# A written-out order for all four compute engines in the RWKV-7 stage of an encoder trunk

## The chip, the cores and the metric

One core of a Trainium2 chip runs the whole program in one launch. The metric is device time in microseconds from start to end of an execution; the median of three runs stands for the kernel.

## What is computed

Two layers on a sequence of 256 tokens of width 1024. Layer 0 mixes tokens by a bidirectional RWKV-7 recurrence, layer 1 by dilated attention; each is followed by a mixture of 32 experts of which a token uses two. Every sub-layer is normalised, shifted, scaled and gated by vectors that are products of c with large matrices (the modulations). The change touches layer 0's recurrence alone:

```python
xx = 0.5 * (x_prev + x_next) - h
xs = h[:, :, None, :] + xx[:, :, None, :] * mu          # six mixes: r, k, v, w, a, g
r, k, v = xs[..., 0..2] @ w_rkv
decay, a, g = low-rank functions of xs[..., 3..5], one for each direction
def step(state, inp):                                   # 16 heads of 64, forward and backward
    sa = einsum('bhvk,bhk->bhv', state, a_t)
    state = state * w_t + sa * b_t + v_t * k_t
    y_t = einsum('bhvk,bhk->bhv', state, r_t)
o = sum over directions of g * (groupnorm(y) + bonus);  out = o @ w_o
```

## The kernel before

**Stages.** Input loads and the first modulations; normalisation and the mixes; the recurrence (`rwkv`); the experts of layer 0, whose 96 weight blocks of 1 MB stream in; attention; the experts of layer 1.

**The recurrence.** 16 heads go as 8 head pairs (index i), both directions (z) at once, in four chunks of 64 tokens. For a pair: the products k, r and v (`keys`, `values`) as three fp16 matmuls each in place of one fp32, from weights and mixes that ACT and DVE or POOL have split into a high and a low half (`split`, `w16`, `halves`, L441 to L449); `rates` (decay and in-context rate); `scale_keys` (two scans L857, BK L880, AR L887 and L888); `chunks` (the matrices G, evicted by DVE as GV and GI, L920; Ah on ACT and Al on POOL, L931 and L932; BT, R2, UV; `bonus`, sT); `inverse` (a triangular inverse by doubling in PSUM banks "iv": PE, then ACT's T and X at L992, then DVE's Q at L1014, six levels); `recur` (four steps R, U, S, Y in banks "ch"); `finish` (group norm by a root of nine small DVE instructions, L345 to L354; yn L1162; oT L1163). Buffers such as AR, GI, BT and UV exist twice (pools `odd` and `even`), so pair i waits for pair i-2.

**What sets the order.** Each of these is a Python generator. `weave` runs them as streams with one clock of its own, `now`, to which it adds an estimate of PE's work; a stream yields the time it thinks it must wait; among ripe streams the one of lowest `RANK` goes next. Within the stage PE's instructions keep the order in which they are made (`on_pe`, `tc.keep_in_program_order`). DVE, ACT and POOL are ordered by the compiling scheduler, by `tc.cur_priority`, which `weave` sets from `now` and `OFFSET`.

**The modulations.** `modulation_flow` takes 48 tiles of 512 KB (`aring`, two slots) and for each adds `w * silu` to `acc` on DVE in two halves of 512 columns (`ada_add`, L374 for the first of eight, L376 for the others), one tile each `PACE` = 4.0 of `weave`'s clock. The loads of `aring` and of the weights (`wring`) are issued by SP in order. When the last pair's products and the modulations are done, `releases` frees pools, in which expert weights are then loaded ahead; more is freed as the last pairs pass.

**The run-up.** Before `weave`: mixes k and r on DVE, the first pair's k and r in fp32, `hidden` with mix w on DVE (pAR) and mix a on ACT and POOL (pUV, L646 and L647), and rates(0). In `weave`, `supply` first does mix v and its split, the splits of k and r, and `hidden_gate` (mix g on ACT and POOL, then 32 hg matmuls).

## Time and profile before

| | us |
|---|---|
| median of three runs (lowest, highest) | 1209.1 (1204.81, 1210.89) |
| the profiled execution: its time | 1205.22 |
| the profiled execution: its span | 1203.4 |
| run-up of the recurrence | 58 to 106 |
| its steady part | 106 to 450 |

Engines: PE = TensorE matmul, PEld = its weight loads, DVE = VectorE, ACT = ScalarE, POOL = GpSimd, SP = SyncE. In the rows below, the page's first part gives busy us, share and instructions; a stretch gives its bounds and length, busy us of each engine with its instructions, PE's mean granted clock, the DMA engines' busy share and GB/s; a group of instructions gives line, engine, operation, tiles, shapes and count, then busy us and mean ns, then the idle time before them and what ended it; a wait gives who waited for whom, us in total, times and the longest; a tile's or line's instructions give their shortest, median and longest duration in ns and their first and last start in us; the timeline gives start, duration, instruction and count, merged where equal ones follow each other, with the idle time before in brackets. A PE that is busy here isn't at its peak, since ends of matmuls are modelled.

### The profile page before, as it was taken

Reading aid. Unit: us, or ns where it says so; the run is one execution under the profiler, and the core shown is the slowest. Engines: PE = TensorE matmul, PEld = TensorE weight load, DVE = VectorE, ACT = ScalarE, POOL = GpSimd, SP = SyncE. Lnnn points to the kernel's source line nnn. Section 1 sums busy time; section 2 is a strip of 40 time slices with the busy share of each in tenths; the row PEclk is TensorE's granted clock in tenths of the full one; section 3 lists DMA queues with packets and bytes.
Section 4 is the critical chain, followed back from the end, with each engine's and each line's share of the span. In section 5 each row is a group of like instructions: output and inputs, shape, how many; then the busy total and the mean of one; then the engine's idle time right before and its main releaser. Section 6 shows DMA issues by size and latency. Waiting matters only on the chain.

```text
span 1203.4 us, 25449 instructions
## 1 busy us (share of the span) xinstructions
PE 1008.3 (84%) x10740; PEld 678.5 (56%) x10740; DVE 674.5 (56%) x1446; ACT 469.0 (39%) x955; POOL 219.7 (18%) x142
## 2 busy tenths in 40 slices
PE   4639778898787989878988989899879999789886
PEld 4527566776565654533433368677768754344432
DVE  6895886687877644412221177988985663122112
ACT  3555565665555442100010176555454631010002
POOL 4472122311312320000000023112292100000000
PEclk9969898988889998998999989998999999899989
DMA  9444344134414287898999996878653599989995
GB/s 368 145 157 146 128 129 137 63 112 145 146 54 142 111 337 282 351 419 352 421 422 420 419 419 233 308 268 327 228 174 130 213 357 373 417 367 421 421 422 223
DMA packets 53199, 322.05 MB, mean 268 GB/s; under 512 B 5922, under 2 KB 6562, under 8 KB 21458
## 3 DMA queue, kind: packets, MB, share of 16 engines
q1 hardware_dynamic: 51986, 315.88, 67.4%
q0 software_dynamic: 800, 3.36, 0.7%
q8 instruction: 89, 1.46, 0.5%
q10 hardware_dynamic: 288, 1.05, 0.3%
q14 instruction: 36, 0.29, 0.1%
HBM read 319.22 MB, written 1.05 MB: 266 GB/s over the span
## 4 chain that ended last, share of the span: by engine, by line
PE 50%; DVE 26%; DMA 12%; ACT 6%; issue 4%; SPq 0%; POOL 0%; ACTq 0%; DVEq 0%; POOLq 0%
PE gu L271 9%; PE qkv L271 8%; DMA wring<-in_w_moe_dram 7%; DVE acc L376 5%; DMA aring<-in_w_ada_dram 5%; PE dn L271 4%; PE xT L271 4%; PE acc L271 4%; PE wo L271 4%; PE iv L271 3%; DVE wl L449 2%; PE kr L271 2%; PE ada L271 2%; PE warm L271 1%; DVE BK L880 1%
## 5 line engine op out<-in xcount | busy, mean ns | idle before, releaser
L271 PE MATMUL gu<-wring,xT 128*32 128x512 f32 x1024 | 134.1, 624 | 15.6 <-DMA wring<-in_w_moe_dram 11.0
L376 DVE SCALAR_TENSOR_TENSOR acc<-aring,silu,acc 128x512 f32<-128x512 f32 x140 | 125.4, 932 | 15.6 <-DMA aring<-in_w_ada_dram 15.3
L443 POOL TENSOR_TENSOR wl<-wring,wh 128x1024 f16<-128x1024 f32 x24 | 57.0, 2379 | 413.0 <-DMA wring<-in_w_qkv_dram 247.1
L271 PE MATMUL qkv<-hh,wl 128*128 128x256 f16 x384 | 106.3, 277 | 2.0 <-DVE wl L449 2.0
L271 PE MATMUL qkv<-hh,wh 128*128 128x256 f16 x384 | 106.4, 277 | 1.8 <-ACT hh L1758 1.8
L271 PE MATMUL qkv<-hl,wh 128*128 128x256 f16 x384 | 106.0, 277 | 1.8 <-DVE hl L1759 1.8
L271 PEld LDWEIGHTS gu<-wring,xT 128*32 128x32 f32 x1024 | 31.2, 113 | 100.3 <-issue 91.1
L449 DVE SCALAR_TENSOR_TENSOR wl<-wring,wh 128x1024 f16<-128x1024 f32 x56 | 74.3, 1330 | 16.9 <-ACT wh L445 16.8
L271 PEld LDWEIGHTS <-wh 128*128 128x128 f16 x768 | 76.4, 100 | 12.9 <-issue 3.5
L271 PE MATMUL dn<-wring,hidT 128*32 128x256 f32 x1024 | 64.5, 398 | 18.5 <-ACT hidT L1561 18.4
L271 PE MATMUL acc<-y,back 128*128 128x512 f32 (+1 forms) x144 | 67.8, 595 | 10.3 <-DVE y L1588 8.1
L1363 DVE SCALAR_TENSOR_TENSOR sg<-sg,gu 128x256 f32<-128x256 f32 x16 | 6.7, 420 | 121.5 <-ACT sg L1362 121.5
L445 ACT ACTIVATE wh<-wring 128x1024 f16<-128x1024 f32 x56 | 58.6, 1050 | 35.8 <-PE qkv L271 28.3
L271 PEld LDWEIGHTS xT<-oh,x 128*128 128x128 f32 x512 | 59.0, 192 | 21.1 <-PE gu L271 9.2
L1588 DVE TENSOR_TENSOR y<-dn,ga 128x512 f32<-128x512 f32 x28 | 19.4, 692 | 89.3 <-PE dn L271 60.1
L1362 ACT ACTIVATE sg<-gu 128x256 f32<-128x256 f32 x16 | 6.1, 384 | 152.7 <-PE gu L271 152.7
L271 PE MATMUL xT<-oh,x 128*128 128x128 f32 x512 | 63.5, 280 | 2.5 <-DVE oh L1472 2.5
L271 PEld LDWEIGHTS dn<-wring,hidT 128*32 128x32 f32 x1024 | 31.4, 113 | 48.4 <-ACT hidT L1561 22.2
L1504 ACT ACTIVATE back<-bT 128x256 f32<-128x256 f32 x16 | 6.2, 386 | 132.0 <-PE acc L271 132.0
L271 PEld LDWEIGHTS <-w 128*128 128x128 f16 x528 | 50.9, 102 | 10.3 <-issue 0.5
L271 PE MATMUL qkv<-wl,hh 128*128 128x256 f16 x192 | 53.3, 278 | 1.3 <-POOL wl L443 1.3
L271 PE MATMUL qkv<-wh,hl 128*128 128x256 f16 x192 | 53.4, 278 | 0.0
(356 smaller groups left out, 2214.8 us busy)
## 6 DMA issues: line engine op xcount, KB each, us to landing
wring<-in_w_moe_dram SPq DMA_DIRECT2D x192, 1024.0 KB, 19.8
aring<-in_w_ada_dram SPq DMA_DIRECT2D x96, 512.0 KB, 4.1
wring<-in_w_qkv_dram SPq DMA_DIRECT2D x36, 1024.0 KB, 9.2
wring<-in_w_kr_dram SPq DMA_DIRECT2D x8, 1024.0 KB, 5.8
wring<-in_w_vl_dram SPq DMA_DIRECT2D x8, 640.0 KB, 4.5
wring<-in_w_rwo_dram SPq DMA_DIRECT2D x4, 1024.0 KB, 6.2
wring<-in_w_ato_dram SPq DMA_DIRECT2D x4, 1024.0 KB, 6.9
x<-in_x_dram POOLq DMA_DIRECT2D x2, 512.0 KB, 7.7
```

The lines of the kernel that those rows point to most:

```text
L271: return on_pe(nc.tensor.matmul(out=o, lhsT=lhsT, rhs=rhs, start=start, stop=stop, **kw))
L376: V.scalar_tensor_tensor(out=acc[:, s], in0=w[:, s], scalar=silu[:, k:k + 1], in1=acc[:, s], op0=ALU.mult, op1=ALU.add)
L443: eng.tensor_tensor(out=lo, in0=src, in1=hi, op=ALU.subtract)
L445: A.activation(out=hi, in_=src, func=AF.Copy, scale=by)
L449: V.scalar_tensor_tensor(out=lo, in0=src, scalar=by, in1=hi, op0=ALU.mult, op1=ALU.subtract)
L880: V.tensor_tensor(out=BK[:, :, par::2, o:o + 64], in0=src.rearrange("p z (c t) -> p z c t", c=4)[:, :, par::2], in1=e2[:, :, par::2], op=A ...
L1362: A.activation(out=o, in_=ps[:, 0:256], func=AF.Tanh, scale=0.5)
L1363: V.scalar_tensor_tensor(out=o, in0=o, scalar=1.0, in1=ps[:, 0:256], op0=ALU.add, op1=ALU.mult)
L1504: A.activation(out=back, in_=ps[:, 0:S], func=AF.Copy)
L1588: V.tensor_tensor(out=y, in0=py[c], in1=gates[i, 5][:, c * 512:(c + 1) * 512], op=ALU.mult)
```

## The change

It replaces `RANK`, `OFFSET` and `weave`'s one clock by an account: for each engine the time at which it is free, for each tile when it was written and by whom, for each PSUM bank when it was last read. DVE, ACT and POOL are wrapped, so that inside `weave` each of their instructions, too, keeps the order in which it is made. A stream yields the engine and the tiles or banks that its next step needs; `weave` runs the step that can start first by the account. An instruction of DVE, ACT or POOL costs a fixed part and a part for each column (`COST`, in microseconds), a hand-over to another engine `HAND`. The account holds no loads.

Besides, work is moved. Mix w goes from DVE to ACT and POOL. Of each modulation tile DVE keeps one half, and POOL does the other with two instructions (one for the first of eight), no earlier than 4n + 2 on the account's clock. The splits become a stream of their own (`conversions`), the gate's mix and matmuls another that begins when the splits of xk and of kr's second half are done; pair 0's v is an fp32 product. Pairs 1 and later wait for the gate before GI. `inverse` begins after Ah (`matrices`) and not after all of `chunks`; sT comes last. Y leaves `recur` for a stream with a bank "yy"; "ch" has one bank left. The load of g1 comes after kr 1.

```diff
-RANK = dict(X=0, C=1, R=2, F=3, D=4, G=5, S=6, H=6, W=7, A=2.5)
-OFFSET = dict(X=0, C=-6, R=-4, F=-2, D=-2, G=-1, S=0, H=0, W=0, A=8)
+GIVE_WAY = dict(X=0, C=0, R=0, D=0.1, Y=0.2, F=0.3, G=0, K=0, S=0.1, B=0.3, H=0, W=0.5, A=0.3)
+COST = dict(V=(0.16, 0.00105), A=(0.19, 0.0008), P=(0.15, 0.00217))
+HAND = dict(T=0.3, V=0.15, A=0.15, P=0.15)
+SWITCH = 0.1
...
+    def account(e, t, outs, ins):
+        start = free[e]
+        for n in ins:
+            w = wrote.get(n)
+            if w:
+                start = max(start, w[0] + (0.0 if w[1] == e else HAND[w[1]]))
+        for n in outs:
+            w = wrote.get(n)
+            if w and w[1] != e:
+                start = max(start, w[0] + HAND[w[1]])
+        free[e] = end = start + t
...
+            def call(*args, **kw):
+                i = f(*args, **kw)
+                if pinned[0]:
+                    tc.keep_in_program_order(i)
...
+                        a, b = COST[self.e]
+                        n = max(int(np.prod(v.shape[1:])) for v in outs)
+                        account(self.e, a + b * n, [v.tensor.name for v in outs], [v.tensor.name for v in ins])
...
         while live:
+            best = None
             for s in live:
...
+                t = start_of(s)
+                if t is None:
+                    continue
+                v = t + GIVE_WAY[s[1]] - (SWITCH if s is last and s[3][0] == "T" else 0.0)
+                if best is None or v < best[0]:
+                    best = (v, t, s)
...
-        ctx2.enter_context(banks(pp=2, ps=2, iv=2, ch=2))
+        ctx2.enter_context(banks(pp=2, ps=2, iv=2, ch=1, yy=1))
...
-                if j in (4, 5):
+                if j in (3, 4, 5):
+                    yield ("A",)
                     A.activation(out=out[k], in_=xx[:, k], func=AF.Copy, scale=mu)
                     P.tensor_tensor(out=out[k], in0=out[k], in1=h[:, k], op=ALU.add)
...
         def hidden_gate():
-            xg, _ = passing(5, "BT")
+            nonlocal oT
+            yield after(("half", 1), ("conv", 1))
+            _, xg = place_of((odd, "GI"), (odd, "BT"))
+            yield from mix_steps(5, xg)
...
+        def first_values():
+            yield after(("room", 2))
+            xv = [v[:, k * S:(k + 1) * S] for v in f32v for k in range(4)]
+            yield from mix_steps(2, xv)
...
+            for k in range(KD):
+                mm(ps[:, 0:S], wv[:, k], xv[k], start=(k == 0), stop=(k == KD - 1))
...
+            yield after(("hidden_gate", 0 if i else -1))
             GI = turns(i, [128, 2, 2, 4, 64], "GI")
...
-            yield after(("ready", i))
-            yield 1.0
+            yield after(("matrices", i))
+            yield ("V", A16[2 * (i % 2)])
...
-            for i, m, k in ADA_RWKV:
+            for n, (i, m, k) in enumerate(ADA_RWKV):
                 w = modulations.take((i, m, k))
...
-                ada_add(acc, w, k, k == 0)
-                yield PACE
+                for e, by in ((1, V), (0, P)):
+                    yield (by.e, PACE * n + 2.0)
+                    a, v = acc[e], w[:, e * 512:e * 512 + 512]
+                    if k == 0:
+                        by.tensor_scalar(out=a, in0=v, scalar1=silu[:, k:k + 1], scalar2=None, op0=ALU.mult)
+                    elif e:
+                        V.scalar_tensor_tensor(out=a, in0=v, scalar=silu[:, k:k + 1], in1=a, op0=ALU.mult, op1=ALU.add)
+                    else:
+                        P.tensor_scalar(out=v, in0=v, scalar1=silu[:, k:k + 1], scalar2=None, op0=ALU.mult)
+                        P.tensor_tensor(out=a, in0=v, in1=a, op=ALU.add)
...
-        streams = dict(X=releases(), C=recurrences(), R=inverses(), F=finishes(), D=readies(), G=last_gates(),
-                       S=supply(), W=outputs(), A=modulation_flow())
+        streams = dict(X=releases(), C=recurrences(), R=inverses(), D=readies(), Y=results(), F=finishes(),
+                       G=last_gates(), K=conversions(), S=supply(), B=hidden_gate(), W=outputs(), A=modulation_flow())
```

## Rows read from the trace of the kernel before

**Rows 1.** The page: span, and busy us (share) of each engine.

```profile
span 1203.4 us, 25449 instructions
PE 1008.3 (84%) x10740; PEld 678.5 (56%) x10740; DVE 674.5 (56%) x1446; ACT 469.0 (39%) x955; POOL 219.7 (18%) x142
```

**Rows 2.** Busy time by stretch: run-up, steady part, expert stage.

```profile
58.00:106.00 48.00, 26.47 (x175) 21.61 (x175) 45.00 (x62) 21.47 (x38) 30.14 (x19) 0.75 0.47 165
...
106.00:450.00 344.00, 290.02 (x5078) 223.12 (x5077) 245.35 (x563) 198.11 (x411) 82.69 (x56) 0.91 0.38 133
...
500.00:520.00 20.00, 18.52 (x172) 9.21 (x168) 5.11 (x14) 2.55 (x7) 0.00 (x0) 1.00 1.01 422
```

**Rows 3.** The chain of waits from 106 to 450 us, shares by line.

```profile
by line: DVE acc L376 9.4%; PE iv L271 9.0%; DMA aring<-in_w_ada_dram 7.1%; PE kr L271 6.0%; issue 5.0%; PE wo L271 3.5%; DVE BK L880 3.4%; PE ada L271 3.2%; DVE Q L1014 3.0%; PE R L271 2.7%; PE S L271 2.5%; PE G L271 2.3%; PE v L271 2.0%; 
```

**Rows 4.** Groups of DVE instructions from 106 to 450 us.

```profile
L376 DVE SCALAR_TENSOR_TENSOR acc<-aring,silu,acc 128x512 f32<-128x512 f32 x70 | 60.5, 892 | 9.2 <-DMA aring<-in_w_ada_dram 8.9
...
L374 DVE TENSOR_SCALAR acc<-aring,silu 128x512 f32<-128x512 f32 x10 | 6.0, 626 | 0.0
```

**Rows 5.** Who waited for whom, from 58 to 476 us.

```profile
PE iv L271 <- DVE Q L1014: 14.8, 9, 4.0
...
DVE acc L376 <- DMA aring<-in_w_ada_dram: 10.9, 10, 2.0
...
PE R L271 <- DVE SD L1092: 8.4, 8, 2.6
```

**Rows 6.** Shortest, median and longest duration of four DVE instructions, their starts.

```profile
L376 DVE SCALAR_TENSOR_TENSOR acc<-aring,silu,acc x70: 736/747/2600, 137.9 to 396.3; 128x512 f32<-128x512 f32 x70
...
L1003 DVE TENSOR_TENSOR X<-Ah,cst x8: 412/426/2353, 103.4 to 415.6; 128x512 f16<-128x512 f16 x8
...
L880 DVE TENSOR_TENSOR BK<-kd,e x16: 416/420/1483, 83.2 to 387.8; 128x256 f32<-128x256 f32 x16
...
L920 DVE TENSOR_TENSOR GV<-G,cstr x32: 409/416/429, 92.2 to 409.7; 128x256 f32<-128x256 f32 x32
```

**Rows 7.** The timeline of the run-up, 46 to 94 us.

```profile
46.37 10.66 POOL L647 TENSOR_TENSOR pUV<-pUV,hT 128x256 f32<-128x256 f32 x8 [9.50 <-ACT pUV L646]
...
52.28 7.30 DVE L649 SCALAR_TENSOR_TENSOR pAR<-xx,colr,hT 128x256 f32<-128x256 f32 x7
...
71.89 1.23 PE L271 MATMUL L<-hidw,wring 64*128 64x256 f32 x4 [7.78 <-DVE kss L793]
...
87.92 5.77 PE L271 MATMUL hg<-pBT,wring 128*128 128x256 f32 x16
```

**Rows 8.** A group of POOL instructions from 58 to 476 us.

```profile
L566 POOL TENSOR_TENSOR wring<-wring,ga 128x512 f32<-128x512 f32 x16 | 21.7, 1390 | 34.8 <-DMA wring<-in_w_rwo_dram 34.8
```

**Rows 9.** The POOL group without an input, whole span.

```profile
L721 POOL MEMSET eb<- 128x528 f32 x1 | 0.5, 537 | 8.1 <-DVE pUV L376 8.1
```

**Rows 10.** The timeline of DVE and of POOL near 346 us.

```profile
345.76 1.48 DVE L880 TENSOR_TENSOR BK<-kd,e 128x256 f32<-128x256 f32 x1
347.17 1.48 DVE L880 TENSOR_TENSOR BK<-bb,e 128x256 f32<-128x256 f32 x1
...
343.95 5.82 POOL L566 TENSOR_TENSOR wring<-wring,ga 128x512 f32<-128x512 f32 x4 [14.67 <-DMA wring<-in_w_rwo_dram]
```

**Rows 11.** Loads of the modulation tiles, issue to landing.

```profile
DMA to landing us min/median/max: 3.4/3.7/4.7
```

**Rows 12.** SP's timeline: first expert loads, first attention loads.

```profile
412.69 13.03 SPq L153 DMA_DIRECT2D wring<-in_w_moe_dram  x8
...
668.65 10.26 SPq L153 DMA_DIRECT2D wring<-in_w_qkv_dram  x5
```

More of the change, by code (lines that the diff above doesn't have):

```diff
@@ L293, in weave @@
+            assert best, (now, [(s[1], s[3]) for s in live], {k: [(n, wrote.get(n), read.get(n)) for n in v[-3:]] for k, v in slots.items()})
+            _, now, s = best
+            step_end[0] = now
+            tc.cur_priority = base + int(20 * now)
             r = next(s[0], "end")
+            last = s
             if r == "end":
@@ L1253, in outputs @@
             yield from out_first()
-            blocks = [gated(b, gates[0, 2], 2).rearrange("p (k n) -> p k n", k=2)
-                      for b in stream.take(("rwo", 1, 0), ("rwo", 1, 1))]
-            last_rows.append(blocks[1])
-            yield after(("inverse", 7), ("finish", 5))
-            yield 4.0
+            two = stream.take(("rwo", 1, 0), ("rwo", 1, 1))
+            for w in two:
+                yield from gating(w, gates[0, 2], 2)
+                blocks2.append(w.rearrange("p (k n) -> p k n", k=2))
@@ L1326, in releases @@
             later(1)
-            yield after(("inverse", 7), ("recur", 6), ("finish", 6), ("gates", 0))
+            yield after(("inverse", 7), ("outputs", 6), ("finish", 6), ("gates", 0))
             inv.release()
```

613 lines of the change are left out of this document (397 added, 216 removed).

## The prediction

> **What bounds the kernel now.** I read the page first, then busy time by stretch, then the chain of waits, then the DVE and POOL groups. The page has TensorE (PE) at 84% of a span of 1203.4 us and DVE at 56% [rows 1], but these are means over unlike stages. By stretch: from 58 to 106 us, the run-up of the recurrence stage, DVE is busy 45.0 of 48 us and PE 26.5; from 106 to 450 us, its steady part, PE is busy 290.0 of 344 us at a mean granted clock of 0.91, DVE 245.4, POOL 82.7; from 500 us the expert weights move at 422 GB/s with the DMA engines full [rows 2]. The change lies in the first two. Of the steady part's chain, 9.4% is the DVE instruction that accumulates the modulations (acc, L376) and 7.1% the load in front of it (aring): together 16.5% of 344, 57 us, for work that the recurrence doesn't need. Inverse matmuls have 9.0% [rows 3]. acc and its first form (L374) take 60.5 + 6.0 us of DVE [rows 4]. The waits say the same of order: PE's inverse waited 14.8 us for DVE's Q, its R product 8.4 us for DVE's SD, and DVE stood 10.9 us at the head of its queue for aring [rows 5]. So the steady part is a full PE held up by a DVE whose queue has unurgent work in front of urgent work.
>
> The unit of the sum is one head pair. Its first DVE step of the inverse (X, L1003) runs 8 times, first at 103.4 and last at 415.6 us [rows 6], a pitch of 312.2/7 = 44.6 us. Scaled from [rows 2], one pair takes 37.6 us of PE (290.0/344), 31.8 of DVE, 10.7 of POOL; 8.6 of DVE's is modulation (66.5/344), 23.2 the rest.
>
> **Run-up.** In the window before 103 us, DVE does the eight mixes xw in 7.30 us; PE then waits 7.78 us for DVE's kss; sixteen hg matmuls take 5.77 us between the two halves of G; POOL's eight mixes take 10.66 us [rows 7]. The change sends xw to ACT and POOL and hg behind the first pair: at best 7.8 + 5.8 = 13.6, some 14 us off. Against it, POOL gets eight more mixes (1.33 us each from its 10.66, 10.7 us) and half of the modulation. It was busy 30.1 of 48 us [rows 2], so 18 us are free; about 12 steps in 48 us at 2.1 us (below) are 25 us, and 10.7 + 25 - 18 = 18 us too many. Conversions and the gate's mixes (xg) queue behind that, so the gain can vanish: bounds +1 and -14, I take **-8 us**, nearer the gain, as only the second pair waits for xg. The fp32 product v for pair 0 is at most as long as those sixteen hg matmuls and falls where PE has 21 us idle: nothing.
>
> **While modulations flow.** 48 steps, step n not before 4n + 2 on the account's clock, fill 192 us from about 58: up to 250 us, of which 147 us (3.3 pairs) are steady. Per pair that is 11 steps. DVE keeps one half of each: 11 x 0.747 = 8.2 us. POOL gets per step one two-input instruction (1.39 us, as wring L566 of that shape) and one scaling in place [rows 8]. The trace has no such scaling; it is bounded below by a fill of 528 columns, 0.54 us [rows 9], and above by the two-input form, 1.39. I take 0.7, near the fill, since it reads one tensor and not two. So 2.1 us a step (1.9 to 2.8), 23 us a pair (21 to 31), beside 7.9 of its own (10.7 less the 21.7 us of wring, which come later): POOL is busy 66 to 87% of a pair, I take 70%.
>
> That share matters, for DVE and POOL shut each other out. BK takes 0.42 us in the median but 1.48 while POOL gates wring; POOL's four take 5.82 us meanwhile [rows 10]. acc goes from 0.747 to 2.600, X from 0.426 to 2.353, whereas GV, which reads PSUM, stays within 0.409 to 0.429 [rows 6]. The price of a meeting: acc's mean lies 0.145 above its median, 10.2 us over 70; POOL is busy 24% of that time, so 17 meet it, at 0.60 us each.
>
> The Trainium skill ("SBUF — State Buffer", Who interferes with whom) says that a DVE instruction with two SBUF inputs and a GpSimd instruction that reads SBUF exclude each other, the second to issue blocking fully. The rows of BK and GV agree; by that rule alone the slower rival below is what happens.
>
> The Trainium skill ("GPSIMD Engine Reference", 3.1 Elementwise) gives 1.03 cycles an element at one or two operations; at its 1.2 GHz that is an estimate of 0.44 us for the scaling, and by it POOL's share would be at my lower end.
>
> In one pair the code has 18 wide DVE instructions of the kinds that meet POOL (two scans, L, WC, kd, two bb, four BK, three AR, X, Ah, w, YT), 18 small ones in the two reciprocal roots, and 11 of modulation. Without meetings DVE needs 23.2 - 18 x 0.24 x 0.60 = 20.6, plus 8.2, so 28.8 us. At 70%, 29 wide ones cost 29 x 0.70 x 0.60 = 12.2: 41.0 us. The small ones cost between nothing (a chain slips through once the port is free) and 18 x 0.70 x 0.60 = 7.6: 48.6. I take nothing, with a pitch of 43.0 us, DVE at 95%: 1.6 us a pair, **-5 us** over 3.3. Bounds: no meetings, PE decides at 39.7 (next part), -16; 48.6, +13.
>
> SP's queue is crossed too: the load of step n+2 now waits for POOL's half. Two slots at 4 us a step give 8 us; landing takes up to 4.7 [rows 11] and POOL 2.1 to 2.8: it fits by under a microsecond. When POOL is late, SP holds the next kr and vl loads behind it, and DVE and POOL stand at their queues' heads for aring.
>
> **After the modulations.** 312 - 147 = 165 us, 3.7 pairs. DVE falls to 23.2 us; PE's 37.6 decides, and it idles 7.0 of 44.6 now. The chain's 57 us would be 7.4 a pair, more than there is. I take 70% of the 7.0, a pitch of 39.7: PE's waits for Q and SD are steps of one chain and won't all be covered. 3.7 x 4.9 = **-18 us**; bounds 0 and -26. The finer streams work here: the inverse starts at Ah and not after sT, R2 and UV; Y leaves the recurrence's loop. They shorten a latency that two buffer sets already overlap, so they count in this term alone. One ch bank for two costs nothing, as R, U and S of a chain are each read before the next is written.
>
> **What follows.** The expert loads begin at 412.7 us and those of attention at 668.7 [rows 12]; their first issues hang on buffers that the last pairs free, so the later stages shift with the stage's end. I count no gain or loss there.
>
> Sum: -8 - 5 - 18 = -31; 1203.4 - 31 = 1172.4. The median of the runs, 1209.1, lies 5.7 above the profiled span: **1178 us**.
>
> **Rivals.**
> *The port decides (slower).* DVE's need passes 44.6 us a pair once meetings cost over 15.8 (44.6 - 28.8); at 48.6 they do. For it: DVE and POOL both run in a fixed order that knows nothing of meetings, so what is blocked also blocks what stands behind it, Q and SD included, and Al behind modulation on POOL. Against: meetings were 10 us for all acc so far. Price: run-up +1, +13 while modulations flow, -4 after (POOL catches up late): +10, **1219 us**.
> *PE's floor.* Few meetings: -14 - 16 - 26 = -56, **1153 us**. For it: PE, DVE and ACT orders from one account; stretches at the lower granted clock would shrink too. Against: [rows 10].
> *The order does nothing.* The account has no loads, no port, no clock; where it is wrong a fixed order stands still, as DVE did for aring in [rows 5]. The gain of 31 goes into such waits: **1209 us**. For it: PE's order was fixed before too, and it idles 54 us in the steady part.
>
> **How the numbers follow.** Forecast 0.53, PE's floor 0.17, port 0.17, nothing 0.13. A measurement of this kernel tells about 0.5% (6 us) from no change. Faster 0.53 + 0.17 = 0.70; same 0.13; slower 0.17. The forecast's own spread is 1163 to 1195; the range, 1150 to 1218, reaches PE's floor and most of the port's case.
>
> **What would show it.** X from 103 to 416 us should become about 95 to 385; pitch near 43, then near 40. POOL's scaling near 0.7 us, its share to 250 us near 70%. BK's and acc's means well above their medians while modulations flow; GV still 0.42. The last acc should come near 250 us and not at 396 [rows 6]. Wrong if the pitch doesn't fall after they end, if BK's and X's means don't rise, or if the expert loads don't begin some 30 us earlier.

## The result, and the profile after

The changed kernel took 1252.9 us in the median of four runs (1249.1 to 1255.1), the kernel before 1207.0 beside it: ratio 1.038, 95% interval 1.033 to 1.042. It is slower by some 46 us where 31 us less were forecast. Its profiled execution has a span of 1249.4 us against 1203.4 [rows 1].

The page of the changed kernel, span and busy us:

```profile
span 1249.4 us, 25556 instructions
PE 1030.5 (82%) x10732; PEld 693.9 (56%) x10732; DVE 666.7 (53%) x1389; ACT 474.7 (38%) x962; POOL 358.9 (29%) x240
```

Busy time by stretch, same columns as [rows 2] (us, then PE, PEld, DVE, ACT, POOL, granted clock, DMA share, GB/s):

```profile
58.00:106.00 48.00, 26.91 (x275) 19.98 (x274) 31.65 (x49) 25.56 (x36) 32.68 (x19) 0.69 0.25 88
106.00:450.00 344.00, 273.91 (x4339) 213.08 (x4340) 227.70 (x470) 183.40 (x375) 198.52 (x132) 0.84 0.36 122
...
193.00:360.00 167.00, 130.72 (x2204) 104.10 (x2204) 115.61 (x226) 90.92 (x185) 117.67 (x74) 0.84 0.40 133
360.00:457.00 97.00, 85.95 (x1612) 66.90 (x1612) 67.22 (x172) 59.44 (x129) 22.39 (x18) 0.92 0.20 74
```

DVE was to be relieved, and hardly was. It gave up 48 half tiles and eight mixes, some 43 us at the prices of the kernel before (48 x 0.747 + 7.3), but on the page its busy time fell by 8 us only (674.5 to 666.7), while POOL's grew by 139 (219.7 to 358.9). From 106 to 450 us POOL went from 82.7 to 198.5 us; that DVE and PE show less there than in [rows 2] says little, since these 344 us hold fewer pairs now: the last X comes at 456.7 us, not at 415.6.

Where in the stage: DVE's step X marks each head pair. In the changed kernel all wrapped instructions have the line of their helper (L307), PE's another (L349), so tiles tell them apart. Pairs 0, 1, 5 and 7 on the DVE timeline, first after, then before (start us, us), for before the two that [rows 6] leave out:

```profile
95.25 2.23 DVE L307 TENSOR_TENSOR X<-Ah,cst 128x512 f16<-128x512 f16 x1
193.35 0.80 DVE L307 TENSOR_TENSOR X<-Ah,cst 128x512 f16<-128x512 f16 x1
388.10 1.38 DVE L307 TENSOR_TENSOR X<-Ah,cst 128x512 f16<-128x512 f16 x1
456.68 0.42 DVE L307 TENSOR_TENSOR X<-Ah,cst 128x512 f16<-128x512 f16 x1
```

```profile
152.70 2.35 DVE L1003 TENSOR_TENSOR X<-Ah,cst 128x512 f16<-128x512 f16 x1
330.55 0.43 DVE L1003 TENSOR_TENSOR X<-Ah,cst 128x512 f16<-128x512 f16 x1
```

With the first expert product (gu, 491.7 us before, 540.0 after, 494.8 in m_dve below) the span falls into six parts that sum to it:

| part, us | before | after | m_dve |
|---|---|---|---|
| start to X of pair 0 | 103.4 | 95.3 | 98.1 |
| X of pair 0 to 1 | 49.3 | **98.1** | 74.9 |
| X of pair 1 to 5 | 177.9 | **194.7** | 168.2 |
| X of pair 5 to 7 | 85.0 | 68.6 | 83.1 |
| X of pair 7 to the experts | 76.1 | 83.3 | 70.4 |
| the rest | 711.7 | 709.4 | 711.6 |

The differences after - before are -8.2, +48.8, +16.9, -16.4, +7.2 and -2.3, in sum +46.0. The loss stands between the first and the second pair, and is as large as the whole; what the next four pairs lose the last two give back. X of pair 1 came at 152.7 us before, at 173.0 in m_dve and at 193.4 after, so one half of its delay is there without POOL's half of the modulation.

The four pairs from X of pair 1 to X of pair 5, same columns, first before, then after:

```profile
152.70:330.55 177.85, 149.24 (x2628) 118.62 (x2626) 134.58 (x317) 109.89 (x226) 42.70 (x26) 0.90 0.37 121
193.35:388.10 194.75, 156.69 (x2618) 125.27 (x2617) 134.34 (x280) 108.44 (x220) 126.00 (x79) 0.84 0.37 123
```

DVE is busy 33.6 us a pair in both, with 280 instructions in place of 317. A pair takes 48.7 us where it took 44.5, and no engine is busy for more than 81% of it: the time lies in waits.

What POOL does: its groups from 58 to 480 us (busy us, mean ns, then idle before), and the shortest, median and longest of the scaling:

```profile
L307 POOL TENSOR_SCALAR aring<-aring,silu 128x512 f32<-128x512 f32 x42 | 78.2, 1863 | 11.9 <-DMA aring<-in_w_ada_dram 10.9 <-DVE acc L307 0.6
L307 POOL TENSOR_TENSOR acc<-aring,acc 128x512 f32<-128x512 f32 x42 | 56.3, 1341 | 3.5
...
L307 POOL TENSOR_SCALAR acc<-aring,silu 128x512 f32<-128x512 f32 x6 | 10.0, 1664 | 7.6 <-DMA aring<-in_w_ada_dram 4.5 <-PE ada L349 3.1
```

```profile
L307 POOL TENSOR_SCALAR aring<-aring,silu x42: 1559/1960/2635, 72.0 to 358.5; 128x512 f32<-128x512 f32 x42
L307 POOL TENSOR_TENSOR acc<-aring,acc x42: 1260/1270/1842, 74.0 to 360.5; 128x512 f32<-128x512 f32 x42
```

A modulation step costs POOL 1.86 + 1.34 = 3.2 us, not 2.1. The scaling in place, with one tensor input, takes 1.56 us at the least, more than the addition of two tensors (1.26); the last step is at 360 us and not at 250.

What that does in the run-up, on POOL's timeline (start us, us; the idle time before in brackets):

```profile
113.74 1.32 POOL L307 TENSOR_TENSOR pGI<-pGI,hT 128x256 f32<-128x256 f32 x2 [0.69 <-ACT pGI L307]
115.04 1.57 POOL L307 TENSOR_SCALAR aring<-aring,silu 128x512 f32<-128x512 f32 x1
116.69 1.26 POOL L307 TENSOR_TENSOR acc<-aring,acc 128x512 f32<-128x512 f32 x1
122.01 0.64 POOL L307 TENSOR_TENSOR pGI<-pGI,hT 128x256 f32<-128x256 f32 x1 [4.06 <-ACT pGI L307]
122.63 1.56 POOL L307 TENSOR_SCALAR aring<-aring,silu 128x512 f32<-128x512 f32 x1
124.28 1.26 POOL L307 TENSOR_TENSOR acc<-aring,acc 128x512 f32<-128x512 f32 x1
...
126.80 2.59 POOL L307 TENSOR_TENSOR pBT<-pBT,hT 128x256 f32<-128x256 f32 x4
```

pGI and pBT are the gate's mixes: 5.3 us of work spread over 15.6 us with modulation between. Behind them stand the gate's products on PE, the third split (vl) and the values of pair 1:

```profile
134.58 3.64 PE L349 MATMUL hg<-pGI,wring 128*128 128x256 f32 x8
...
148.21 0.28 PE L349 MATMUL v<-xv,w 128*128 128x256 f16 x1
```

In the kernel before the gate's products began at 87.9 us [rows 7], in m_dve below at 118.8. From 58 to 106 us POOL begins only five modulation steps and is busy 32.7 of 48 us; nine more begin between 109 and 147 us, in the second pair's way. The chain of waits from X of pair 0 to X of pair 1, by line, first after, then before, then m_dve:

```profile
by line: DMA aring<-in_w_ada_dram 16.3%; POOL aring L307 11.1%; issue 9.4%; PE kr L349 7.7%; POOL acc L307 7.1%; DMA ga<-in_p_adab_dram 5.0%; PE L L349 4.7%; PE v L349 4.5%; DVE rsq L307 2.6%; PE vc L349 2.5%; POOL xr L307 2.2%; POOL xv L30
```

```profile
by line: PE kr L271 16.9%; DVE acc L376 14.3%; DMA aring<-in_w_ada_dram 9.0%; PE iv L271 7.2%; PE v L271 5.7%; issue 5.4%; ACT w L445 4.0%; ACT wring L441 3.8%; ACT UV L953 3.3%; ACT T L992 3.1%; PE R L271 2.3%; PE ada L271 2.3%; PE sT L271
```

```profile
by line: issue 14.5%; PE hg L349 12.5%; PE iv L349 7.1%; DMA ga<-in_p_adab_dram 6.2%; DVE acc L307 5.3%; PE ada L349 3.8%; ACT UV L307 3.5%; PE R L349 3.1%; DVE rsq L307 3.1%; PE L L349 2.7%; DVE rsy L307 2.7%; PE S L349 2.2%; DVE gvar L307
```

After the change the loop of the modulation (load of a tile, POOL's scaling and addition, release of the slot, next load) has 34.5% of 98.1 us of this chain, 34 us. Before, acc and the loads have 23.3% of 49.3, 11 us; in m_dve acc has 5.3% of 74.9, 4 us, but there the gate's products, which in the kernel before stood ahead of pair 0's X, have 12.5%, 9 us. A chain is one path: others as long can stand beside it.

What it does to DVE: its groups from 58 to 480 us, first after, then m_dve (the same orders, without POOL's half):

```profile
L307 DVE TENSOR_TENSOR AR<-kk,eb 128x256 f32<-128x256 f32 x16 | 8.0, 538 | 0.0
L307 DVE TENSOR_TENSOR X<-Ah,cst 128x512 f16<-128x512 f16 x8 | 7.1, 889 | 0.3
L307 DVE TENSOR_TENSOR Ah<-Ah,cst 128x512 f16<-128x512 f16 x8 | 4.4, 553 | 4.8 <-POOL Al L307 4.7
L307 DVE TENSOR_TENSOR rsq<-rsy 128x4 f32<-128x4 f32 x16 | 4.1, 254 | 0.3
```

```profile
L307 DVE TENSOR_TENSOR AR<-kk,eb 128x256 f32<-128x256 f32 x16 | 6.1, 418 | 0.0
L307 DVE TENSOR_TENSOR X<-Ah,cst 128x512 f16<-128x512 f16 x8 | 3.4, 421 | 0.2
L307 DVE TENSOR_TENSOR Ah<-Ah,cst 128x512 f16<-128x512 f16 x8 | 3.4, 420 | 0.7 <-POOL Al L307 0.6
...
L307 DVE TENSOR_TENSOR rsq<-rsy 128x4 f32<-128x4 f32 x20 | 3.2, 162 | 0.3
```

Over all groups outside the modulation with at least eight instructions in both kernels (441 instructions; mean times the smaller count, summed), DVE needs 217.3 us after and 184.6 in m_dve: 33 us for the same work. Counted in the same way against the kernel before (433 instructions) it needs 208.9 and 183.7, 25 us more. That isn't X or BK, whose means were as high before; the rise lies in others such as AR, kd and the small ones. Two lines of before, then one of after:

```profile
L1003 DVE TENSOR_TENSOR X<-Ah,cst 128x512 f16<-128x512 f16 x8 | 7.5, 936 | 0.4
L880 DVE TENSOR_TENSOR BK<-kd,e 128x256 f32<-128x256 f32 x16 | 9.8, 618 | 0.0
```

```profile
L307 DVE TENSOR_TENSOR BK<-kd,e 128x256 f32<-128x256 f32 x16 | 8.6, 534 | 0.0
```

GV, which reads PSUM, stayed at 405 to 426 ns:

```profile
L307 DVE TENSOR_TENSOR GV<-G,cstr x32: 405/414/426, 86.7 to 452.1; 128x256 f32<-128x256 f32 x32
```

Last, DVE's waits from 58 to 500 us (total, times, longest); [rows 5] had 10.9 us here:

```profile
DVE acc L307 <- DMA aring<-in_w_ada_dram: 39.7, 17, 5.2
```

### The profile page after: what moved, and what is told of

Read it like the earlier page. It is cut to its first block, busy times and chain, and to the rows that moved or that the text cites. A ratio compares the mean times of both kernels' runs of the same rounds, so it can differ in the third digit from the quotient of the medians.

```text
span 1249.4 us, 25556 instructions
## 1 busy us (share of the span) xinstructions
PE 1030.5 (82%) x10732; PEld 693.9 (56%) x10732; DVE 666.7 (53%) x1389; ACT 474.7 (38%) x962; POOL 358.9 (29%) x240
## 4 chain that ended last, share of the span: by engine, by line
PE 43%; DMA 23%; DVE 21%; ACT 5%; issue 4%; POOL 4%; ACTq 0%; SPq 0%; DVEq 0%; POOLq 0%
DMA wring<-in_w_moe_dram 17%; PE qkv L349 8%; PE gu L349 5%; DMA aring<-in_w_ada_dram 4%; DVE acc L307 4%; PE wo L349 3%; PE kr L349 3%; PE iv L349 3%; PE acc L349 2%; PE xT L349 2%; PE dn L349 2%; POOL aring L307 2%; DVE wl L307 2%; DVE rsq L307 1%; DVE pUV L307 1%
## 5 line engine op out<-in xcount | busy, mean ns | idle before, releaser
L307 POOL TENSOR_TENSOR wl<-wring,wh 128x1024 f16<-128x1024 f32 x24 | 55.9, 2332 | 407.6 <-ACT wh L307 387.7
L349 PE MATMUL gu<-wring,xT 128*32 128x512 f32 x1024 | 133.6, 619 | 17.1 <-DMA wring<-in_w_moe_dram 13.4
L307 DVE SCALAR_TENSOR_TENSOR acc<-aring,silu,acc 128x512 f32<-128x512 f32 x98 | 90.1, 946 | 42.9 <-DMA aring<-in_w_ada_dram 42.7
L349 PE MATMUL qkv<-hh,wl 128*128 128x256 f16 x384 | 106.0, 277 | 2.3 <-DVE wl L307 2.3
L349 PE MATMUL qkv<-hl,wh 128*128 128x256 f16 x384 | 106.0, 276 | 2.0 <-DVE hl L307 2.0
L349 PE MATMUL qkv<-hh,wh 128*128 128x256 f16 x384 | 106.1, 277 | 1.6 <-ACT hh L307 1.6
L307 ACT ACTIVATE wh<-wring 128x1024 f16<-128x1024 f32 x80 | 83.8, 1051 | 47.7 <-PE qkv L349 41.9
L349 PEld LDWEIGHTS gu<-wring,xT 128*32 128x32 f32 x1024 | 31.2, 112 | 101.7 <-issue 86.4
L349 PEld LDWEIGHTS <-wh 128*128 128x128 f16 x768 | 76.3, 100 | 13.1 <-issue 3.6
L307 DVE SCALAR_TENSOR_TENSOR wl<-wring,wh 128x1024 f16<-128x1024 f32 x56 | 73.2, 1312 | 16.8 <-ACT wh L307 16.7
L307 POOL TENSOR_SCALAR aring<-aring,silu 128x512 f32<-128x512 f32 x42 | 78.2, 1863 | 11.9 <-DMA aring<-in_w_ada_dram 10.9
L349 PE MATMUL dn<-wring,hidT 128*32 128x256 f32 x1024 | 64.7, 399 | 18.3 <-ACT hidT L307 18.1
L307 DVE SCALAR_TENSOR_TENSOR sg<-sg,gu 128x256 f32<-128x256 f32 x32 | 13.4, 419 | 122.6 <-ACT sg L307 122.2
L349 PE MATMUL acc<-y,back 128*128 128x512 f32 (+1 forms) x144 | 66.0, 581 | 10.3 <-DVE y L307 10.3
L307 DVE TENSOR_TENSOR y<-dn,ga 128x512 f32<-128x512 f32 (+1 forms) x36 | 22.8, 632 | 92.0 <-PE dn L349 62.7
L349 PEld LDWEIGHTS xT<-oh,x 128*128 128x128 f32 x512 | 59.0, 192 | 21.1 <-PE gu L349 9.2
L349 PE MATMUL xT<-oh,x 128*128 128x128 f32 x512 | 63.5, 280 | 2.5 <-DVE oh L307 2.5
L307 ACT ACTIVATE sg<-gu 128x256 f32<-128x256 f32 x16 | 6.1, 384 | 154.3 <-PE gu L349 154.3
L349 PEld LDWEIGHTS <-w 128*128 128x128 f16 x504 | 51.4, 107 | 13.3 <-issue 2.0
L349 PEld LDWEIGHTS dn<-wring,hidT 128*32 128x32 f32 x1024 | 31.5, 114 | 47.7 <-ACT hidT L307 21.9
L307 POOL TENSOR_TENSOR acc<-aring,acc 128x512 f32<-128x512 f32 x42 | 56.3, 1341 | 3.5
L307 ACT ACTIVATE back<-bT 128x256 f32<-128x256 f32 x16 | 6.2, 386 | 130.2 <-PE acc L349 130.2
```

Source lines behind the costliest of these rows:

```text
L307: i = f(*args, **kw)
L349: return on_pe(nc.tensor.matmul(out=o, lhsT=lhsT, rhs=rhs, start=start, stop=stop, **kw), o, lhsT, rhs, t)
```

## The experiments

Each runs beside the kernel before; a ratio is to that.

**Which part of the change loses: m_dve and b_pool.** m_dve is the changed kernel with both halves of the modulation on VectorE; b_pool is the kernel before with POOL's half and nothing else of the change.

```diff
 m_dve (on after)
-for e, by in ((1, V), (0, P)):
+for e, by in ((1, V), (0, V)):
 b_pool (on before)
-ada_add(acc, w, k, k == 0)
+columns 512..1023: V.scalar_tensor_tensor; columns 0..511: P.tensor_scalar in place, P.tensor_tensor
```

> The changed kernel with one part undone: DVE does both halves of every modulation tile, POOL none. If POOL's half is what costs (its queue full in the run-up, the port shared with DVE later), X of pair 1 comes back from 193 us to 150 or earlier, the pitch to about 43, and the time falls to between 1175 and 1210 us. If the new streams and the fixed orders cost by themselves, it stays above 1235.

> The kernel before with that one part added: POOL scales and adds one half of every modulation tile, all else as it was. If POOL's half costs by itself, 1235 to 1255 us. If it costs only under the new order, within 1% of before, 1207.

m_dve: 1211.2 us, ratio 1.001 (0.998 to 1.004). b_pool: 1248.3 us, 1.033 (1.028 to 1.037). POOL's half is the whole loss, and it costs the old order about as much as the new one. X of pair 1 in m_dve came at 173.0 us and not by 150, though. Without POOL's half the new orders and streams come out even: the table's last column shows 9.6 us gained from pair 1 to 5 (42.1 us a pair against 44.5) and 25.7 lost between the first two pairs.

**Where the run-up's loss comes from: m_late, m_dlate, m_gate, m_best.**

```diff
 m_late (on after), m_dlate (on m_dve)
-yield (by.e, PACE * n + 2.0)
+yield (by.e, PACE * n + 70.0)
 m_gate (on m_dve): g1 loaded before kr 1; the gate waits for ("half", 1), ("fp32v", 0) alone; conversions wait for the gate
 m_best (on m_dve): as m_gate, but conversions wait for the taking of g1 alone
```

> The changed kernel with the modulations' earliest times moved from 4n + 2 to 4n + 70 on the account's clock: the same work on POOL, but none in the run-up. If POOL's queue in the run-up costs the 41 us, X of pair 1 comes near 150 us; the slow pitch of 48.7 then comes in the pairs after it, and the gain of the last two pairs is lost: 1215 to 1235 us. If the new streams cost it, X of pair 1 stays near 190 and the time near 1250.

> The changed kernel with both halves of the modulation on VectorE and with the floor of modulation step n put at 4n + 70 us of the account instead of 4n + 2. Two earlier runs showed the pieces: with VectorE alone X of pair 1 stands at 173 us and the later pitch is 41.9 us; with the late floor (and POOL's half) X of pair 1 stands at 163 us. Theory one (the run-up loses because modulation work stands ahead of the small operations of the first pairs, whoever does it): X of pair 1 at about 163 us, pitch 42 us, last X near 414 us, so 10 us less than with VectorE alone, ratio 0.988 to 0.996. Theory two (the run-up's delay is of the loads, the gate's g1 and the ring's slots, not of the modulations): X of pair 1 stays near 172 us and the ratio is 1.00. Theory three (the work that is moved out of the run-up is paid for later one for one): X of pair 1 falls but the pitch rises to 44 us, ratio 1.00.

> m_dve with the gate's stream put back where it was: g1 is loaded before kr 1, the gate waits for xk's split and pair 0's v only, and the splits of kr 1 wait for the gate. If the gate's new place costs m_dve its run-up (X of pair 1 at 173 us and not 153), X of pair 1 comes to about 150 and the time to between 1185 and 1200 us. If it is something else in the run-up, X of pair 1 stays near 173 and the time near 1211.

> The changed kernel with both halves of the modulation on VectorE, and with the hidden layer of the gate put back to its place in the kernel before: its weights are loaded ahead of the second pair's key weights, it waits for the first key split and the first values alone, and (unlike the earlier run that moved the gate) the key weights of pair 1 are split while the gate runs, not behind it; the third split of pair 1 still stands behind the gate. In the run with VectorE alone the gate's products stood at 118.8 to 130.1 us and the third split began at 128.7, so the values of pair 1 came at 137.8 us (118.1 before) though its keys came at 107.3 us (114.5 before). Theory one (the run-up's loss under the new order is this chain: gate, third split, values of pair 1): gate near 88 us, values of pair 1 near 120 us, X of pair 1 at 155 to 160 us, all later pairs 10 to 15 us earlier than with VectorE alone, ratio 0.985 to 0.994. Theory two (in the run-up the engines' own time is the limit, and a link of the chain that is shortened is replaced by the next): X of pair 1 at 168 to 173 us, ratio 0.998 to 1.003. Theory three (the earlier gate delays pair 0): X of pair 0 above 100 us, ratio above 1.003.

m_late: 1248.0 us, 1.033 (1.028 to 1.039), not 1215 to 1235: X of pair 1 came at 163.0 us instead of 193.4, but the later pitch was 47.8 us and the last X came at 449.8 (456.7 after). m_dlate: 1227.1 us, 1.017 (1.014 to 1.020): X of pair 1 at 159.3 us (173.0 in m_dve) and yet 0.016 of the ratio, some 19 us, slower than m_dve; the last X is at 426.4 instead of 424.4, and the experts begin at 518.5 instead of 494.8, where the modulations end at 435 us instead of 384. So modulation work in the run-up does delay the second pair, as the first theory had it, but what is moved out of the run-up is paid for later and more than one for one, which none of the three theories had.

m_gate: 1209.1 us, 1.000 (0.997 to 1.004): the gate's products came back to 88.6 us, but the keys of pair 1 moved from 107.3 to 132.9 us and X of pair 1 stayed at 171.3. One link replaced another. m_best: 1222.6 us, 1.015 (1.010 to 1.019): the edit missed its aim. The gate's products stayed at 121.7 us, since ACT's part of the last mixes came late, as the last line of POOL's timeline before them shows:

```profile
118.73 1.32 POOL L306 TENSOR_TENSOR pBT<-pBT,hT 128x256 f32<-128x256 f32 x2 [7.65 <-ACT pBT L306]
```

So it doesn't test its theory, and the 20 us by which the second pair is late even in m_dve are not settled. It does show that a small edit of the waits can shift the time by 1.4%, so differences of this size between two orders need not have the cause that was edited.

**What the fixed orders are worth: m_free.** m_dve with only PE pinned.

```diff
 if pinned[0]:
-    tc.keep_in_program_order(i)
```

> m_dve in which DVE, ACT and POOL are not held to the order of the source; PE still is, and the account and the priorities are the same. If the fixed orders of the three give the shorter pitch (41.9 us against 43.8 before), the pitch rises to 43 or more and the time to 1220 or more. If they give nothing, within 0.5% of m_dve, 1211.

1223.3 us, 1.016 (1.011 to 1.020), against 1.001 for m_dve: the orders of DVE, ACT and POOL are worth some 1.4% to these streams. The pitch rose to 42.6 us only, not to 43; X of pair 1 came 6.5 us later.

**Is it the scaling's price: m_cost and m_act.** m_cost gives the account the scaling's measured 1.56 us; m_act moves the 42 scalings to ACT.

```diff
 m_cost
-a, b = COST[self.e]
+a, b = (0.15, 0.00275) if self.e == "P" and name == "tensor_scalar" else COST[self.e]
 m_act
-P.tensor_scalar(out=v, in0=v, scalar1=silu[:, k:k + 1], ...)
+A.activation(out=v, in_=v, func=AF.Copy, scale=silu[:, k:k + 1])
```

> The changed kernel with one number of the account put right: a POOL scaling of 512 columns costs 1.56 us in it, as the trace has it alone, and not 1.26. If the loss is POOL's load, 1245 to 1258 us. If it is that the fixed order rests on a wrong price, 1215 or less.

> The changed kernel with one instruction per modulation step moved: the one-input scaling of POOL's half runs on ScalarE instead (an activation with the column of silu as scale), and POOL keeps the first tile's scaling of each part and the 42 additions. Question: is it the mis-sized scaling (1.56 us alone, 1.86 us on average, where 0.7 us had been estimated) that turned a gain into a loss? POOL's share per step falls from about 3.2 us to about 1.35 us, below the 0.7 + 1.27 = 2.0 us on which the forecast rested, while ScalarE gains 42 x about 0.65 us = 27 us (its 128x512 fp32 activations take 0.63 to 0.69 us). Theory one (the price of the scaling is the failed step; with a cheap POOL half the forecast's steps hold): between 1185 and 1205 us, ratio 0.98 to 0.998, X of pair 1 by 170 us or earlier and the last modulation sum near 300 us. Theory two (any half on POOL loses, because POOL's place in the chain of the splits and its reads of SBUF cost, cheap or not): ratio 1.01 to 1.03, X of pair 1 near 180 us. Theory three (ScalarE, now loaded more, delays the evictions): ratio above 1.03.

m_cost: 1244.0 us, 1.027 (1.023 to 1.031). m_act: 1243.3 us, 1.029 (1.025 to 1.032), with X of pair 1 at 178.8 and the last modulation at 445 us. So each repair gives back 10 to 13 of the 46 us and no more (0.011 and 0.009 of the ratio). In m_cost X of pair 1 came back to 175.3, but the pitch after it was 47.4. For m_act the second theory holds in time and place; its reason isn't tested, for there POOL's additions wait in their fixed place for ACT, which ends the pace as surely as the price did (POOL's waits, 58 to 480 us):

```profile
POOL acc L307 <- ACT aring L307: 57.8, 19, 9.9
```

**How much and where: m_quart, m_post, m_bpost.** POOL keeps its half in the first, third and fifth part (24 of 48 steps), or in the last four parts (32 steps); m_bpost joins m_post and m_best.

```diff
 m_quart
+for e, by in ((1, V), (0, P if m in (0, 2, 4) else V)):
 m_post
+for e, by in ((1, V), (0, P if n >= 16 else V)):
```

> The changed kernel with half of POOL's modulation work given back: POOL takes its half in three of the six parts (the first, third and fifth, 24 of 48 steps), VectorE both halves in the other three. Question: does the loss grow with the amount of POOL's work, or with where it stands? The first part stands in the run-up (40 to 100 us). If the loss is proportional to POOL's work: half of the 3.4 to 3.8%, so ratio 1.015 to 1.02 (about 1229 us). If it is the run-up's part that costs, with POOL busy before the first pair's small operations, nearly all of it stays: ratio above 1.025, X of pair 1 near 190 us as in the changed kernel. If only sustained load costs (POOL falling ever further behind), it is under 1.01.

> The changed kernel with VectorE doing both halves of the modulation in the first two parts (16 of 48 steps, the run-up), and POOL its half in the last four (32 steps, 102 us of POOL's time). It is the counterpart of the run in which POOL kept the first, third and fifth part and which lost 3.0%, with X of pair 1 at 201 us and a later pitch of 42.5 us. Theory one (what costs is POOL's work in the run-up; later POOL has the room and VectorE is freed): X of pair 1 near 173 us as with VectorE alone, pitch 41 to 42 us, ratio 0.99 to 1.003. Theory two (POOL's work costs wherever it stands): X of pair 1 near 173 us, pitch 45 to 49 us, ratio 1.015 to 1.03.

> The gate's place of the run before the last and the division of the last one together: gate early, VectorE alone in the first two parts, POOL's half in the last four. If both first theories hold the gains add: X of pair 1 at 155 to 160 us, ratio 0.975 to 0.99, faster than both kernels. If the second theory of either holds, the ratio is that of the worse of the two less the gain of the other, 1.00 to 1.02.

m_quart: 1245.0 us, 1.030 (1.027 to 1.034), X of pair 1 at 201.4 us and a pitch of 42.4 after it: here the loss is in the run-up. m_post: 1238.8 us, 1.030 (1.023 to 1.036), X of pair 1 at 183.7 and a pitch of 43.4; from the last X to the experts it took 83.2 us against 70.4 in m_dve. Against m_dve the loss is spread: 11 us before pair 1, 9 over six pairs, 13 behind the last. So the second theory has the ratio, though not the pitch of 45 to 49 that it asked for. Half or two thirds of POOL's work cost nearly what all of it does. m_bpost: 1229.6 us, 1.020 (1.015 to 1.026); with m_best at 1.015 it comes out between the two and adds nothing.

**By which mechanism: b_fill and b_read.** The kernel before, with idle POOL work at each modulation step: nine fills of 256 columns, without any read, or four products of 256 columns that read constants.

```diff
 b_fill
+for _ in range(9): P.memset(idle, 0.0)
 b_read
+for _ in range(4): P.tensor_tensor(out=idle, in0=cst[:, 0:256], in1=cst[:, 0:256], op=ALU.mult)
```

> The same with nine POOL fills a step in place of the four that read: about as long on POOL's queue, but nothing is read from SBUF. If the shared port is what costs, about as before, 1205 to 1215 us, and below b_read by 10 us or more. If POOL's queue (Al and the splits standing behind) is what costs, as slow as b_read.

> The kernel before, with four more POOL instructions of 256 columns that read two constants from SBUF (about 0.7 us each, 2.9 a step) added to each of the 48 modulation steps; nothing waits for what they write, and DVE still does all of the modulation. If the shared port is what costs, DVE's two-input instructions stretch and the time is 1222 us or more. If POOL's half costs through its own lateness (loads held, Al late), little changes: 1205 to 1215.

POOL's added group of each, 58 to 480 us:

```profile
L1206 POOL MEMSET idle<- 128x256 f16 x373 | 117.7, 316 | 19.8
```

```profile
L1206 POOL TENSOR_TENSOR idle<-cst 128x256 f16<-128x256 f32 x156 | 107.6, 690 | 10.2
```

b_fill: 1230.7 us, 1.020 (1.016 to 1.023). b_read: 1303.4 us, 1.080 (1.078 to 1.083). b_fill lies between its two cases; b_read is above 1222, as its first case asks, but mostly not by the stretching of DVE's instructions that the case names. A busy POOL queue that reads nothing costs 2.0%: the splits behind it come late (the third split of a weight began at 130.5 us, before at 116.2). Nor does the four times larger loss of b_read show a price of reading, for the compiling scheduler put the idle work elsewhere. POOL's timeline in b_read, then in b_fill:

```profile
29.17 27.50 POOL L1206 TENSOR_TENSOR idle<-cst 128x256 f16<-128x256 f32 x33
...
57.11 12.35 POOL L1206 TENSOR_TENSOR idle<-cst 128x256 f16<-128x256 f32 x16
69.42 0.82 POOL L649 TENSOR_TENSOR pUV<-pUV,hT 128x256 f32<-128x256 f32 x1
...
139.64 19.24 POOL L1206 TENSOR_TENSOR idle<-cst 128x256 f16<-128x256 f32 x28
158.83 1.15 POOL L934 TENSOR_TENSOR Al<-GV,Ah 64x512 f16<-64x512 f32 x1
```

```profile
46.14 4.89 POOL L649 TENSOR_TENSOR pUV<-pUV,hT 128x256 f32<-128x256 f32 x1 [4.12 <-ACT pUV L648]
...
105.80 1.15 POOL L934 TENSOR_TENSOR Al<-GV,Ah 64x512 f16<-64x512 f32 x1
```

In b_read 40 us of idle products stand ahead of mix a, which begins 23 us later than in b_fill and in the kernel before [rows 7], and another 19 us of them stand ahead of pair 0's Al. X of pair 0 came at 162.3 us (108.9 in b_fill, 103.4 before), X of pair 1 at 243.0 (171.1 and 152.7): these 90 us are as much as its profiled execution lost in all (87.7), and the pitch after them is 43.4 us (45.5 and 43.8). So b_read, too, shows mostly the queue, at another place. What reads cost stands in DVE's durations alone: its common groups, counted as above, rise by 6 us under fills and by 11.5 under reads.

**Taking the links away: m_qdve, m_qfree, m_split, m_qsplit.** m_qfree moves the recurrence's own POOL work (second halves of the splits, Al) to VectorE, so that little stands behind modulation in POOL's queue; m_qdve is its control without POOL's half. m_split gives each engine its own slots for its half of a tile, POOL's loaded by POOL's queue; m_qsplit joins m_qfree and m_split.

```diff
 m_qfree (on after), m_qdve (on m_dve)
-yield from parting(h, l, v, XSC, P)
+yield from parting(h, l, v, XSC, V)
-yield from parting(t[:, 0], t[:, 1], src, WSC, V if j == 2 else P)
+yield from parting(t[:, 0], t[:, 1], src, WSC, V)
-P.tensor_tensor(out=l, in0=a, in1=h, op=ALU.subtract)
+V.tensor_tensor(out=l, in0=a, in1=h, op=ALU.subtract)
 m_split (on after)
-modulations.lengthen(apool, 2, len(modulations.plan))
+ringv = Stream(nc.sync, apool, [(a, ap["w_ada"][a][:, 512:1024]) for a in ADA_RWKV], 2, 512, "aringv")
+ringp = Stream(P, apool, [(a, ap["w_ada"][a][:, 0:512]) for a in ADA_RWKV], 2, 512, "aringp")
```

> The changed kernel with POOL's half of the modulation kept, but with the recurrence's own POOL work given to VectorE: the second halves of the splits of keys, rates and inputs (18 + 2 instructions of 128x1024, 2.1 to 2.5 us each on POOL, 1.24 us on VectorE) and of the inverse's start (16 of 64x512, 1.22 us on POOL), 67 us off POOL and about 32 us onto VectorE. POOL then does little but modulation, and nothing that PE waits for stands behind it. Question: is it the queue on POOL (splits behind modulation) or POOL's reads of SBUF beside VectorE that costs 3.8%? Theory one (the queue): X of pair 1 back to 175 us or earlier, ratio at most 1.005. Theory two (VectorE is slowed by POOL's reads, wherever POOL's work comes from): the added DVE work comes on top, ratio 1.03 to 1.06. The run beside it, without POOL's half, gives the price of moving the splits alone.

> Control for the run beside it: the same moved splits, and both halves of the modulation on VectorE, so that POOL does nearly nothing in the recurrence and VectorE about 32 us more than with VectorE alone. If VectorE's time decides: X's pitch 41.9 + 32 / 8 = 46 us, ratio 1.02 to 1.03. If the splits' path decides (1.24 us on VectorE in place of 2.3 us on POOL, and 0.4 in place of 1.25 us twice a pair in the inverse's start) and VectorE has the room (251 of 344 us busy): ratio 0.985 to 1.00.

> The changed kernel, its division and its orders kept, with the ring of modulation tiles parted: in place of two slots of 128x1024 that VectorE and POOL both have to release, two slots of 128x512 for VectorE (loaded by SP's queue as before) and two for POOL (loaded by POOL's own queue, one more DMA issue of about 0.6 us on POOL a step). The room in SBUF and the bytes are the same. Question: every run with a half on POOL showed VectorE waiting 31 to 67 us for the landing of the next tile (9 to 25 us without), with SP's queue waiting for POOL to release the slot. Theory one (the shared slot carries POOL's slowness to VectorE, where the fixed order queues the recurrence's own work behind the wait): VectorE's wait for its tiles falls to 10 to 20 us, X of pair 1 near 175 us, ratio 1.00 to 1.02. Theory two (the wait on the tile is only where slowness shows; POOL's queue and its reads are the cause): the wait falls, but the ratio stays at 1.03 to 1.045. Theory three (the DMA issues on POOL add 29 us to its queue and the splits suffer more): ratio above 1.045.

> The two last edits together: the recurrence's splits and the inverse's start on VectorE (as in m_qfree, so that nothing PE waits for stands in POOL's queue) and the ring of modulation tiles parted (as in m_split, so that VectorE doesn't wait for POOL's release of a slot). What POOL's half can still do to the others is its traffic beside VectorE. The control is m_qdve (1243.5 us, ratio 1.031), where VectorE does both halves. m_qfree, with the shared slots, stood 27 us above it, and VectorE waited 67 us for modulation tiles. Theory one (those 27 us are the shared slot): VectorE's wait for tiles under 20 us, and with 42 us less work on VectorE the time is at or below the control's: ratio 1.00 to 1.03. Theory two (the 27 us are POOL's traffic beside VectorE): the wait falls, but the ratio stays at 1.045 to 1.055, and VectorE's instructions that are not modulation have longer means than in the control.

m_qdve: 1243.5 us, 1.031 (1.026 to 1.036), so moving the splits alone costs 3%; X of pair 1 came at 191.0 us, with a pitch of 45 after it. m_qfree: 1270.6 us, 1.051 (1.045 to 1.057), with X of pair 1 at 192.3: the second theory. POOL's half still costs 27 us with nothing of the splits behind it, less than the some 43 us between the changed kernel and m_dve (0.037 of the ratio). m_split: 1248.0 us, 1.036 (1.032 to 1.040): the second theory. m_qsplit: 1257.1 us, 1.042 (1.038 to 1.045), between its theories. DVE's wait for its tiles, 58 to 480 us, in m_qfree, m_split and m_qsplit:

```profile
DVE acc L307 <- DMA aring<-in_w_ada_dram: 67.2, 30, 4.8
```

```profile
DVE acc L307 <- DMA aringv<-in_w_ada_dram: 12.7, 9, 3.0
```

```profile
DVE acc L307 <- DMA aringv<-in_w_ada_dram: 23.9, 19, 3.3
```

In m_split the wait fell by 27 us and the time by at most a few, with X of pair 1 at 191.6. But POOL's own queue had 27.2 us of DMA issues more (46 of 0.59 us, which the account prices at 0.1), so a gain from the parted slots and a loss in that queue can have cancelled: what the shared slot costs the changed kernel isn't shown. In m_qsplit, where nothing of the splits hangs on POOL's queue, parting the slots gives back about half of the 27 us (0.010 of the ratio). The other half (1257.1 - 1243.5 = 13.6) remains although VectorE does half the modulation only and waits no longer for its tiles than in m_qdve (23.9 us against 25.2); its common groups stand at 236.0 us against 212.2 there. That fits POOL's traffic beside it, but no run isolates it. So two links are shown to cost time where they stand alone: POOL's queue (24 us in b_fill) and the shared slot (some 12 us between m_qfree and m_qsplit, 3 to 20 by their intervals). The third, POOL's reads, is shown in DVE's durations (33 us in all) and not in time. They don't add, and how the changed kernel's 43 us part among them stays open. No version tried beats the kernel before.

## Why the prediction was wrong, step by step

- **What bounds the kernel:** that urgent work stands behind unurgent work fits the runs, as m_free, which lets go of the fixed orders, loses 1.4%. That relieving DVE is worth something isn't shown: in m_dve DVE keeps the whole modulation, and yet the pitch from pair 1 to 5 fell to 42.1 us. That this is near the 43.0 forecast for a relieved DVE is luck.
- **Run-up, -8 us: the step that failed.** It was right for pair 0, whose X came at 95.3 us as written (95) and 8.2 earlier than before. But the term ended there. "Nearer the gain, as only the second pair waits for xg" was the wrong choice, since the second pair sets the start of the other seven: up to its X the change costs 40.6 us (48.8 - 8.2), where the bound was +1. One half of that, 20 us, is there without POOL's half (m_dve). On the chain 9 us of it are the gate's products, which no longer stand ahead of pair 0; but putting the gate back (m_gate) gained 2 us only, so the rest of its cause stays open. The other half comes with POOL's half, and not by the term's sum of twelve steps in 48 us: POOL began five by 106 us, and it was the later ones, with their loads, that the second pair waited for (34 us of the chain).
- **The scaling, 0.7 us: mis-sized.** It measured 1.56 at the least and 1.86 in the mean, beyond the bound of 1.39. "It reads one tensor and not two" was the error: a form not in the trace was put near the fill, though the nearest row that reads at all was the two-input form. The change's own price list has 1.26 for it (0.15 + 0.00217 x 512 in `COST`), which the sum passed over. That alone doesn't explain the result: with the scaling on ACT 2.9% remain.
- **While modulations flow, 43.0 us a pair, set by a DVE busy for 41.0 of it: the mechanism failed too.** A pair took 48.7 us with DVE busy for 33.6. That 48.7 meets the 48.6 that was worked out for small instructions meeting POOL is luck, for by that sum DVE would be busy throughout. Small ones are hit (rsq on 128x4 went from 162 to 254 ns), but against the 28.8 us reckoned without meetings DVE's 33.6 leave some 5 us a pair for all of them, where 12.2 were taken. What fills the pair is waiting, as DVE's for its tiles (27.6 us from 193 to 360). POOL's share was 70% from 193 to 360 us, as forecast, but for 360 us and not to 250.
- The Trainium skill ("SBUF — State Buffer", Who interferes with whom) has a DVE instruction with two SBUF inputs and a reading GpSimd instruction exclude each other, and the trace agrees in kind: X had a mean of 889 ns against 421 in m_dve, while GV from PSUM stayed as it was. But X had 936 ns in the kernel before, and BK went from 618 to 534: against that kernel these two means did not rise, which the prediction names as a sign of its being wrong.
- The Trainium skill ("GPSIMD Engine Reference", 3.1 Elementwise) has 1.03 cycles an element at one or two operations, at its 1.2 GHz an estimate of 0.44 us for the scaling; the trace has 1.56 at the least, and the measurement decides.
- **SP's queue, "fits by under a microsecond":** it didn't. DVE waited 39.7 us at its head for tiles, and the loads are the largest item (16.3%) of the chain to the second pair's X. What they cost by themselves isn't shown, as m_split changed POOL's queue as well.
- **After the modulations, 39.7:** 34.3 us a pair at POOL's 22.4 of 97 us busy and a clock of 0.92, better than forecast; but only two pairs were left for it, not 3.7. How much of it is catching up isn't known; m_dve, whose modulations end at 384 us, takes 41.6.
- **Later stages, none:** +4.9 us (7.2 - 2.3), nearly one for one.
- **The rivals:** "the port decides" had the direction and, in the modulated part, the size (+13 against +16.9). Its mechanism, DVE's need above 44.6 us a pair, is not what happened (33.6), and its run-up price of +1 was as wrong as the forecast's. "The order does nothing" is what m_dve measured, once POOL's half is gone.

## What to carry to other kernels

Work that goes to an idle engine is paid for by everything behind it in that engine's queue and by what shares its buffers: test the division alone, on the old order, before an order is built upon it. Sums of busy time don't give the pitch of a pipeline in which no engine is full; its waits do. Idle work put in as a test has to be looked up in the timeline, since a scheduler can place two kinds of it differently. A gain read at the first unit of a pipeline says nothing until the second has come, since a run-up's cost stands between the two. A price that the trace doesn't show belongs near the row that moves the same data, not near the cheapest one.

## What was unexpected of the hardware

On POOL, scaling a 128x512 fp32 tile in place by a column took at least 1.559 us, the sum of two such tiles 1.260. POOL fills, which read nothing, took 316 ns for 128x256 fp16 and still cost the kernel 2.0% at 117.7 us of them.
